# A two-layer decoder trunk on one core: sums of feed-forward weights moved from GpSimd to VectorE, and 13 instead of 15 blocks by the seven-product scheme

## The chip, the cores and the metric

The kernel runs on one core of a Trainium2 chip. The metric is device microseconds of one execution of the whole program, as a median over runs. The engines of the core are named as the profile names them: PE (TensorE, matrix products; PEld is its loading of weights), DVE (VectorE), ACT (ScalarE), POOL (GpSimd), and SP, which here only issues transfers. All engines run their own instruction stream in order and wait for each other by semaphores.

## The reference, cut to what matters

The program computes two decoder layers on a sequence of 512 tokens of width 1024, in float32. Each layer is an attention mixer followed by a feed-forward part, each with a norm in front and a residual added behind. Only the feed-forward part is touched by the change:

```
def rmsnorm(x, g):
    y = xf * lax.rsqrt(jnp.mean(xf * xf, axis=-1, keepdims=True) + NORM_EPS)
    return (y * g.astype(jnp.float32)).astype(x.dtype)

def swiglu(xn, w_gate, w_up, w_down):
    return (jax.nn.silu(xn @ w_gate) * (xn @ w_up)) @ w_down

    for layer in range(DEPTH):
        ...
        h = h + swiglu(rmsnorm(h, ffn_norm_g[layer]), ffn_w_gate[layer], ffn_w_up[layer], ffn_w_down[layer])
    return rmsnorm(h, final_norm_g)
```

The gate and up matrices are 1024 x 2816 each and the down matrix is 2816 x 1024, so a layer has 22 blocks of 128 hidden features.

## The kernel before

Activations lie transposed: 128 features on the partitions, 512 tokens along the free axis. Every float32 operand of a matrix product is held as two parts that the fast matmul type can take: a high part (ACT copies the value into that type) and a low part (DVE subtracts the high part from the value). A product of two such operands is three matmuls: high x high, high x low, low x high (`mm3`, L429; `product`, L919).

The function `ffn` (L851) computes a block of 128 hidden features in one of two ways.

*Direct* (`plain`, L864): for gate and for up, a slab of weights (128 x 1024) is loaded into `wraw`, split into `whl` (high by ACT, low by DVE, 1024 columns each), and multiplied with all eight chunks of the input `xo`: 24 matmuls of 512 columns for each of the two, 48 in all. DVE then scales the gate by the norm's factor `rbc`, ACT applies Silu, DVE multiplies with up, and the result is split into two parts again.

*By seven products* (`winograd`, L926): gate and up together form a 2 x 2 arrangement of blocks (gate and up against the two halves of the 1024 inputs), the input likewise (two halves of the features against two halves of the tokens). Strassen's scheme in Winograd's form needs seven products of half the size instead of eight: p1 to p7, each of 4 chunks x 3 matmuls of 256 columns, 84 matmuls in all. The price is sums. Those of the input are formed once per layer (`sums_of_x`, L884, into `tf`). Those of the weights are formed for each block: `a2` (tile `wu`) is the up slab, to whose first half a transfer adds its second half (L931, issued by POOL); then three POOL instructions of 512 columns each form `s23` (both halves) and `s4` (L939, L941, L944); the trace calls all of these `s`. The operands are then split: `w1` from the gate slab `a1` in `wraw`, `w3` from `s23`, `w2` from `a2` (one half of its low part by a second transfer that adds, L948), all into buffers `whl`, and `w4` from `s4` into `wf`. The products are evicted by one ACT copy and seven DVE additions of 256 columns (`add`, L959), after which come the scaling, Silu and the product of gate and up. The order on PE is p1, p6, p2, p7, p5, p4, p3; p6 and p7 use `w3`.

Before the change the blocks 0 and 1 of each layer are direct, 2 to 16 go by seven products, and 17 to 21 are direct. The results of the first six blocks are split at once into `hd`; the others wait as `hr` until the seven-product blocks are over and are split then (`later`, L986). The down projection follows, eight outputs with 22 x 3 matmuls each.

Buffers set how far ahead the operands can be made: two of `wraw`, four of `whl` (a seven-product block takes three, a direct one two), two of `wf`, three of `wu`, two of `s23`, two of `s4`.

No order of instructions is written by hand. `Sched` (L63) lists all operations with a cost and their dependences, simulates the engines, and writes each engine's stream in the order of that simulation. PE's operations have costs of their own there (`mm`, L356), DVE's are `vtt` (L243), POOL's `gtt` (L251), and the costs of DVE and POOL know nothing of each other.

Of the kernel before, what the change touches and what calls it, by code (L numbers as in the profile page):

```python
# [10 lines left out]
F32 = mybir.dt.float32  # L11
F32R = mybir.dt.float32r
# [3 lines left out]
OP = mybir.AluOpType  # L16
# [46 lines left out]
class Sched:  # L63
# [7 lines left out]
    def buf(self, tag):  # L71
        b = Buf(tag, len(self.queue[tag]))
        self.queue[tag].append(b)
        return b

    def op(self, alts, fn, r=(), w=(), dma=0, late=0.0):
        o = Op(len(self.ops), alts, fn, dma)
        o.late = late
        o.boost = self.boost
        self.ops.append(o)  # L80
        for toks, wr in ((r, False), (w, True)):
            for b, k in toks:
                if not b.ops or b.ops[-1] is not o:
                    b.ops.append(o)
                    o.bufs.append(b)
                lw, rd = b.tok.get(k, (None, []))
                if lw is not None and lw is not o:
                    o.pred.add(lw)
                if wr:
                    o.pred.update(x for x in rd if x is not o)  # L90
                    b.tok[k] = (o, [])
                else:
                    rd.append(o)
                    b.tok[k] = (lw, rd)
        return o
# [119 lines left out]
ENDED = {1: (), 2: (1,), 3: (1,), 4: (1, 3), 5: (1, 2, 3, 4), 6: (1, 2, 3, 4, 5), 7: (1, 2, 3, 4, 5),  # L215
         8: (1, 2, 3, 4, 5, 7)}
CLOSES = {1: (), 2: (1,), 3: (), 4: (3,), 5: (4, 2), 6: (5,), 7: (), 8: (7,)}
NP, NS, ND = 2, 15, 6
ORDER = ("Q0 Q1 A0 V1 Q2 A1 Q3 A2 V2 Q4 A3 Q5 A4 Q6 A5 Q7 V3 A6 A7",
         "Q0 V1 Q1 A0 Q2 A1 Q3 A2 V2 Q4 A3 Q5 A4 Q6 A5 Q7 V3 A6 A7")  # L220
LAT = 150.0
# [38 lines left out]
def trunk(ctx, tc, xT, pos, consts_in, gv, lamv, wv0, wqk0, wo0, wgu0, wd0, wv1, wqk1, wo1, wgu1, wd1, out):  # L260
    nc = tc.nc
    V, A, G, T = nc.vector, nc.scalar, nc.gpsimd, nc.tensor
    E = {"V": V, "A": A, "G": G, "T": T}

    AT, FK, FW, FH = (1, 5), (2, 6), (3, 7), (4, 8)
# [3 lines left out]
    def tag(name, shape, dt, n, scope=0):  # L269
        tags[name] = (scope, n)  # L270
        shapes[name] = (shape, dt)

    R5 = [128, 512]
# [17 lines left out]
    for L in range(2):  # L291
        sc = AT[L]
        for n, shp, dt, c in (("v", [128, 4, 2, 256], F32R, 2), ("sh", R5, F32, 2), ("a", R5, F32, 2),
                              ("kk", [128, 2, 512], F32R, 4), ("qs", R5, F32R, 4), ("lg", R5, F32, 4),
                              ("pt", [128, 2, 1664], F32R, 2), ("of", R5, F32, 1),
                              ("ot", [128, 2, 512], F32R, 8), ("col", [128, 4], F32, 8)):
            tag(f"{n}{L}", shp, dt, c, sc)
        if L == 1:
            tag("ss1", [128, 2, 512], F32R, 1, sc)
        else:  # L300
            tag("ma0", R5, F32, 1, sc)
        for sc, defs in ((FK, (("hd", [128, 2, 512], F32R, ND), ("hr", R5, F32, NP + NS - ND), ("rbc", R5, F32, 1),
                               ("cg", R5, F32, 2), ("cu", R5, F32, 2))),
                         (FW, (("tf", [128, 8256], F32R, 1), ("wf", [128, 2, 512], F32R, 2), ("wu", [128, 1024], F32, 3),
                               ("s23", [128, 1024], F32, 2), ("s4", R5, F32, 2))),
                         (FH, (("hh", [128, 2, 512], F32R, NF - ND),))):
            for n, shp, dt, c in defs:
                tag(f"{n}{L}", shp, dt, c, sc[L])

    S_ = Sched(tags, None)  # L310
    op, buf = S_.op, S_.buf
# [22 lines left out]
    def tt(e_alts, out_, a, b, o, n, r, w):  # L334
        op([(e, vtt(n) if e == "V" else gtt(n)) for e in e_alts],
           lambda e: E[e].tensor_tensor(out_(), a(), b(), o), r, w)  # L336
# [514 lines left out]
    def ffn(L, wgu, wd, gi_next):  # L851


        rbc = None
        ht = {}
# [2 lines left out]

        def parts(f, src, r):

            t = ht[f] = buf(f"hd{L}" if f < ND else f"hh{L}")
            split(lambda: t.t[:, 0, :], lambda: t.t[:, 1, :], src, 512, r, (t, 0), (t, 1), "V")

        def plain(f):  # L864
# [61 lines left out]
        def winograd(f):  # L926
            a1, a2, s23, s4 = buf("wraw"), buf(f"wu{L}"), buf(f"s23{L}"), buf(f"s4{L}")
            A1, A2 = wgu[2 * f], wgu[2 * f + 1]
            k1, k2 = slice(0, 512), slice(512, 1024)
            dma(lambda: a2.t, lambda: A2, (), [(a2, 0), (a2, 1)], 2 ** 19)  # L930
            op([("G", 1100)], lambda e: G.dma_start(a2.t[:, k1], A2[:, k2], accum_op=OP.add), [(a2, 0)], [(a2, 0)],  # L931
               dma=2 ** 19, late=4500.0)
            dma(lambda: a1.t, lambda: A1, (), [(a1, 0), (a1, 1)], 2 ** 19)
            w1, w3, w2, w4 = buf("whl"), buf("whl"), buf("whl"), buf(f"wf{L}")
            halves = lambda t: [(t, 0), (t, 1)]
            both = lambda w, src, n, r: split(lambda: w.t[:, 0, :], lambda: w.t[:, 1, :], lambda: src.t, n, r,
                                              (w, (0, 0)), (w, (1, 0)), "V")
            both(w1, a1, 1024, halves(a1))
            tt("G", lambda: s23.t[:, k1], lambda: a2.t[:, k1], lambda: a1.t[:, k1], OP.subtract, 512,  # L939
               [(a2, 0), (a1, 0)], [(s23, 0)])  # L940
            tt("G", lambda: s23.t[:, k2], lambda: a2.t[:, k2], lambda: s23.t[:, k1], OP.subtract, 512,  # L941
               [(a2, 1), (s23, 0)], [(s23, 1)])
            both(w3, s23, 1024, halves(s23))
            tt("G", lambda: s4.t, lambda: s23.t[:, k1], lambda: a1.t[:, k2], OP.subtract, 512, [(s23, 0), (a1, 1)],  # L944
               [(s4, None)])
            copy("A", lambda: w2.t[:, 0, :], lambda: a2.t, 1024, halves(a2), [(w2, (0, 0))])
            copy("A", lambda: w2.t[:, 1, k2], lambda: a2.t[:, k2], 512, [(a2, 1)], [(w2, (1, 1))], scale=-1.0)
            op([("G", 1100)], lambda e: G.dma_start(w2.t[:, 1, k2], A2[:, k2], accum_op=OP.add), [(w2, (1, 1))],  # L948
               [(w2, (1, 1))], dma=2 ** 19, late=4500.0)
            tt("V", lambda: w2.t[:, 1, k1], lambda: a2.t[:, k1], lambda: w2.t[:, 0, k1].bitcast(F32), OP.subtract, 512,  # L950
               [(a2, 0), (w2, (0, 0))], [(w2, (1, 0))])
            both(w4, s4, 512, [(s4, None)])
            p1, p6, p2, p7, p5, p4, p3 = [buf("ps_" + n) for n in "gsgtgos"]
            g, u = buf(f"cg{L}"), buf(f"cu{L}")
            P = lambda p: [(p, None)]
            q = lambda t: (lambda: t.t[:, :256])
            g0, g1, u0, u1 = [lambda t=t, k=k: t.t[:, k] for t in (g, u) for k in (lo_, up_)]

            def add(dst, a, p, tok, rd, o):  # L959
                tt("V", dst, a, q(p), o, 256, P(p) + rd, [tok])  # L960
            product(p1, w1, 0, xb(0, 0))
            copy("A", u0, q(p1), 256, P(p1), [(u, 0)], psum=True)
            product(p6, w3, 0, xt(1))
            add(g1, u0, p6, (g, 1), [(u, 0)], OP.add)
            product(p2, w1, 512, xb(1, 0))
            add(g0, u0, p2, (g, 0), [(u, 0)], OP.add)
            product(p7, w3, 512, xt(2))
            add(u0, g1, p7, (u, 0), [(g, 1)], OP.add)
            product(p5, w2, 0, xt(0))
            add(u1, u0, p5, (u, 1), [(u, 0)], OP.subtract)  # L970
            add(g1, g1, p5, (g, 1), [], OP.subtract)
            product(p4, w2, 512, xt(3), 1)
            add(u0, u0, p4, (u, 0), [], OP.add)
            product(p3, w4, 0, xb(1, 1))
            add(g1, g1, p3, (g, 1), [], OP.subtract)
            tt("V", lambda: g.t, lambda: g.t, lambda: rbc.t, OP.mult, 512, [(rbc, None)], halves(g))
            func(lambda: g.t, lambda: g.t, AF.Silu, 512, SET, [(g, 0), (g, 1)])
            if f < ND:
                tt("V", lambda: u.t, lambda: u.t, lambda: g.t, OP.mult, 512, halves(g), halves(u))
                parts(f, lambda: u.t, halves(u))  # L980
                return
            t = buf(f"hr{L}")
            tt("V", lambda: t.t, lambda: u.t, lambda: g.t, OP.mult, 512, halves(g) + halves(u), [(t, None)])
            return lambda: parts(f, lambda: t.t, [(t, None)])

        later = []  # L986
        for f in range(NF):
            if f == NP + NS:
                for x in later:
                    x()  # L990
            if f < NP or f >= NP + NS:
                plain(f)
                if f == 0:
                    sums_of_x()
            else:
                x = winograd(f)
                if x is not None:
                    later.append(x)
# [12 lines left out]
        for n in range(NC):  # L1011
# [9 lines left out]
            t = buf(f"cu{L}")  # L1021
# [213 lines left out]
```

## Time and profile before

| what | us |
|---|---|
| median of three runs | 1225.76 (1225.22 to 1231.3) |
| the profiled execution, its own time | 1226.0 |
| span of that execution, first to last instruction | 1224.1 |
| PE busy in the span | 1185.5 (97%) |
| DVE busy | 868.9 (71%) |
| ACT busy | 685.7 (56%) |
| POOL busy | 344.6 (28%) |
| gate and up products of layer 0, first direct block to last seven-product block | 253.39 to 438.64 |
| the same in layer 1 | 853.78 to 1035.81 |

The shares of the whole span are averages over stages with different limits. The change lies in two stretches of it, the two in the last rows, and those have to be read by themselves: what PE does there one product after another (the timeline), what the other engines are busy with in the same stretch (the windows), how long one and the same instruction takes at different moments (the instructions of a line), and what an idle engine waited for (the waits).

### The profile page before, as it was taken

The numbers are of one execution on the slowest core, as the hardware profiler recorded it, in microseconds if no ns is written. First come the engines' busy times: TensorE is split into PE (matmuls) and PEld (weight loads), VectorE is DVE, ScalarE is ACT, GpSimd is POOL, SyncE is SP. The second block draws the span as 40 slices with busy tenths as digits, with TensorE's granted clock in tenths as the row PEclk, the third lists the DMA queues.
The fourth block names the chain that finished last, engine by engine and source line by source line (L and its number), as shares of the span: only waits on it lengthen the run. The fifth ranks groups of instructions, "written<-read, shape, count | busy, mean of one in ns | idle before, by whom it ended". The sixth has DMA issues, their size and how long they took to land.

```text
span 1224.1 us, 19042 instructions
## 1 busy us (share of the span) xinstructions
PE 1185.5 (97%) x7074; PEld 1046.9 (86%) x7074; DVE 868.9 (71%) x1675; ACT 685.7 (56%) x1207; POOL 344.6 (28%) x292
## 2 busy tenths in 40 slices
PE   9999999998999999999999899999999999999997
PEld 7889788888999988888898787888899999888887
DVE  7876896679999974333246888975999999533333
ACT  7777987664454453222357788986745445432221
POOL 1222332255565400000021425322646561000000
PEclk9999999999999999999999999999999999999998
DMA  8775764554666443333578557555456663333322
GB/s 255 183 157 130 171 146 109 133 145 105 156 155 149 111 116 96 95 97 99 128 184 193 127 136 161 134 135 140 122 145 154 147 155 105 103 95 95 97 76 70
DMA packets 55916, 162.43 MB, mean 133 GB/s; under 512 B 6800, under 2 KB 10000, under 8 KB 55824
## 3 DMA queue, kind: packets, MB, share of 16 engines
q1 hardware_dynamic: 38832, 116.08, 30.7%
q0 software_dynamic: 16704, 45.10, 22.0%
q8 instruction: 56, 0.92, 0.3%
q14 instruction: 36, 0.29, 0.1%
q10 hardware_dynamic: 288, 0.04, 0.0%
HBM read 150.71 MB, written 2.10 MB: 125 GB/s over the span
## 4 chain that ended last, share of the span: by engine, by line
PE 49%; issue 21%; DVE 21%; DMA 4%; ACT 3%; POOL 1%; SPq 0%; DVEq 0%; POOLq 0%; ACTq 0%
PE ps_g L358 35%; PE ps_s L358 6%; DVE whl L336 5%; PE ps_o L358 3%; PE ps_t L358 3%; DVE cg L336 3%; DMA kk<-kk 2%; DVE cu L336 2%; PE ps_t L361 2%; DVE hr L336 2%; DVE lg L723 1%; DVE wf L336 1%; DVE lg L339 1%; DMA h<-xT 1%; DVE kk L336 1%
## 5 line engine op out<-in xcount | busy, mean ns | idle before, releaser
L358 PE MATMUL ps_g<-xo,whl 128*128 128x512 f32 (+1 forms) x2112 | 439.1, 356 | 0.0
L358 PEld LDWEIGHTS ps_g<-xo,whl 128*128 128x128 f32 x2112 | 346.4, 189 | 49.2
L327 ACT ACTIVATE whl<-wraw 128x1024 fp32r<-128x1024 f32 (+1 forms) x218 | 222.9, 1039 | 257.8 <-PE ps_g L358 181.9
L336 DVE TENSOR_TENSOR whl<-wraw,whl 128x1024 fp32r<-128x1024 f32 (+1 forms) x106 | 145.5, 1373 | 87.8 <-ACT whl L327 87.5
L358 PE MATMUL ps_g<-hh,whl 128*128 128x512 f32 (+1 forms) x816 | 177.7, 377 | 0.0
L358 PEld LDWEIGHTS ps_g<-hh,whl 128*128 128x128 f32 x816 | 146.9, 188 | 28.0
L358 PE MATMUL ps_g<-whl,xo 128*128 128x256 f32 x672 | 93.1, 288 | 0.0
L358 PEld LDWEIGHTS ps_g<-whl,xo 128*128 128x128 f32 x672 | 87.4, 193 | 1.3
L353 ACT ACTIVATE cg<-cg 128x512 f32<-128x512 f32 x44 | 27.6, 628 | 99.2 <-DVE cg L336 99.2
L353 ACT ACTIVATE lg<-lg,col 128x128 f32<-128x128 f32 (+3 forms) x128 | 70.8, 554 | 10.2 <-DVE col L723 9.0
L358 PE MATMUL ps_g<-ot,whl 128*128 128x512 f32 x288 | 73.6, 396 | 0.0
L396 POOL DMA_DIRECT2D whl<-wv x14 | 12.3, 879 | 200.8 <-ACT whl L327 199.8
L358 PE MATMUL ps_g<-hd,whl 128*128 128x512 f32 (+1 forms) x306 | 68.6, 377 | 0.0
L358 PE MATMUL ps_s<-kk,qs 128*128 128x128 f32 (+3 forms) x256 | 62.7, 327 | 5.2 <-DMA kk<-kk 4.7
L358 PEld LDWEIGHTS ps_g<-hd,whl 128*128 128x128 f32 x306 | 55.3, 188 | 10.6
L336 DVE TENSOR_TENSOR cu<-ps_g,rbc 128x512 f32<-128x512 f32 (+1 forms) x17 | 11.2, 660 | 72.4 <-PE ps_g L358 72.4
L358 PEld LDWEIGHTS ps_g<-ot,whl 128*128 128x128 f32 x288 | 52.9, 188 | 10.0
L358 PE MATMUL ps_s<-tf,whl 128*128 128x256 f32 x360 | 51.4, 285 | 10.3 <-DVE whl L336 8.5
L396 POOL DMA_DIRECT2D whl<-wqk x30 | 26.3, 878 | 109.9 <-ACT whl L327 72.0
L358 PEld LDWEIGHTS ps_s<-tf,whl 128*128 128x128 f32 x360 | 45.5, 188 | 13.7 <-DVE whl L336 11.5
L336 POOL TENSOR_TENSOR hr<-h,hr 128x256 f32<-128x256 f32 x4 | 2.8, 733 | 190.9 <-ACT hr L327 190.9
L336 POOL TENSOR_TENSOR sh<-sh,sk 128x512 f32<-128x512 f32 x28 | 38.7, 1383 | 60.1 <-DVE sh L682 48.3
(180 smaller groups left out, 2213.5 us busy)
## 6 DMA issues: line engine op xcount, KB each, us to landing
wraw<-wgu SPq DMA_DIRECT2D x58, 512.0 KB, 3.7
wraw<-wd SPq DMA_DIRECT2D x32, 512.0 KB, 3.5
wraw<-wqk SPq DMA_DIRECT2D x30, 512.0 KB, 6.8
whl<-wqk POOLq DMA_DIRECT2D x30, 512.0 KB, 7.4
wu<-wgu SPq DMA_DIRECT2D x30, 512.0 KB, 4.4
kk<-kk SPq DMA_DIRECT2D x64, 128.0 KB, 5.2
wraw<-wo SPq DMA_DIRECT2D x16, 512.0 KB, 5.2
wu<-wgu POOLq DMA_DIRECT2D x30, 256.0 KB, 4.3
```

What stands on the lines that cost most here:

```text
L327: A.activation(out_(), in_(), AF.Copy, scale=sc)
L336: lambda e: E[e].tensor_tensor(out_(), a(), b(), o), r, w)
L339: op([("V", vtt(n, 1))], lambda e: V.scalar_tensor_tensor(out_(), a(), s(), b(), o0, o1), r, w)
L353: A.activation(out_(), in_(), f, scale=scale, **kw)
L358: lambda e: T.matmul(out_(), l(), r_(), start=start, stop=stop), r, w)
L361: op([("T", 108)], lambda e: T.transpose(out_(), in_(), ident()), r + [(cc, None)], w)
L396: op([("G", 1100)], lambda e: G.dma_start(w.t[:, 1, :], src, accum_op=OP.add), [(w, (1, 0))], [(w, (1, 0))], dma=2 * 1024 * 512)
L723: op([("V", vtt(w) + 10)], lambda e: V.tensor_tensor_reduce(lg.t[:, :w], p.t[:, :w], mask[0]()[:, 512 - w:], -0.125, 3.0e38, OP.add, OP.mi ...
```

## The change

It does two things. The three sums of weights of a seven-product block (`s23`, both halves, and `s4`) are formed by DVE instead of POOL. And the blocks 2 and 9 of each layer are computed directly, so that 13 blocks in place of 15 go by seven products: 3 to 8 and 10 to 16. Six blocks are still split at once into `hd` (now 0 to 4 and 9), and eleven `hr` remain.

```diff
@@ -215,7 +215,10 @@
-NP, NS, ND = 2, 15, 6
+NW = 17
+PLAIN = (0, 1, 2, 9)
+DIRECT = (0, 1, 2, 3, 4, 9)
+ND = len(DIRECT)
@@ -299,7 +302,7 @@
-        for sc, defs in ((FK, (("hd", [128, 2, 512], F32R, ND), ("hr", R5, F32, NP + NS - ND), ("rbc", R5, F32, 1),
+        for sc, defs in ((FK, (("hd", [128, 2, 512], F32R, ND), ("hr", R5, F32, NW - ND), ("rbc", R5, F32, 1),
@@ -858,7 +861,7 @@
-            t = ht[f] = buf(f"hd{L}" if f < ND else f"hh{L}")
+            t = ht[f] = buf(f"hd{L}" if f in DIRECT else f"hh{L}")
@@ -936,12 +939,12 @@
             both(w1, a1, 1024, halves(a1))
-            tt("G", lambda: s23.t[:, k1], lambda: a2.t[:, k1], lambda: a1.t[:, k1], OP.subtract, 512,
+            tt("V", lambda: s23.t[:, k1], lambda: a2.t[:, k1], lambda: a1.t[:, k1], OP.subtract, 512,
                [(a2, 0), (a1, 0)], [(s23, 0)])
-            tt("G", lambda: s23.t[:, k2], lambda: a2.t[:, k2], lambda: s23.t[:, k1], OP.subtract, 512,
+            tt("V", lambda: s23.t[:, k2], lambda: a2.t[:, k2], lambda: s23.t[:, k1], OP.subtract, 512,
                [(a2, 1), (s23, 0)], [(s23, 1)])
             both(w3, s23, 1024, halves(s23))
-            tt("G", lambda: s4.t, lambda: s23.t[:, k1], lambda: a1.t[:, k2], OP.subtract, 512, [(s23, 0), (a1, 1)],
+            tt("V", lambda: s4.t, lambda: s23.t[:, k1], lambda: a1.t[:, k2], OP.subtract, 512, [(s23, 0), (a1, 1)],
                [(s4, None)])
@@ -975,7 +978,7 @@
-            if f < ND:
+            if f in DIRECT:
@@ -985,10 +988,10 @@
-            if f == NP + NS:
+            if f == NW:
                 for x in later:
                     x()
-            if f < NP or f >= NP + NS:
+            if f in PLAIN or f >= NW:
                 plain(f)
```

Since the scheduler writes the streams anew, the order around these instructions moves too; outside the two stretches it is the same on every engine. Three places follow. In the rows `whl`, `wf`, `wu`, `wraw`, `cg`, `cu` and `hr` are the buffers named above, `s_0_2511` and `s_1_2512` are the two buffers of `s23`, `s_0_2513` and `s_1_2514` those of `s4`; `ps_...` are accumulators of the products. Lines behind 218 stand three lower in the changed file (L339 is L336 of before).

DVE, layer 0, one seven-product block in the middle of the stretch, before, from the scaling of the finished block's gate on:

```order
L336 TENSOR_TENSOR cg_0_2497<-cg_0_2497,rbc_0_2496 128x512
L336 TENSOR_TENSOR cg_1_2498<-cu_1_2500,ps_s_85 128x256
L336 TENSOR_TENSOR hr_8_2493<-cu_0_2499,cg_0_2497 128x512
L336 TENSOR_TENSOR cg_1_2498<-cu_1_2500,ps_g_83 128x256
L336 TENSOR_TENSOR whl_73<-s_0_2511,whl_73 128x1024
L336 TENSOR_TENSOR cu_1_2500<-cg_1_2498,ps_t_88 128x256
L336 TENSOR_TENSOR whl_74<-wu_0_2508,whl_74 128x512
L336 TENSOR_TENSOR cu_1_2500<-cu_1_2500,ps_g_84 128x256
L336 TENSOR_TENSOR cg_1_2498<-cg_1_2498,ps_g_84 128x256
L336 TENSOR_TENSOR cu_1_2500<-cu_1_2500,ps_o_89 128x256
L336 TENSOR_TENSOR whl_75<-wraw_71,whl_75 128x1024
L336 TENSOR_TENSOR cg_1_2498<-cg_1_2498,ps_s_86 128x256
```

and in the changed kernel, a block of the same kind:

```order
L339 TENSOR_TENSOR cg_1_2498<-cg_1_2498,rbc_0_2496 128x512
L339 TENSOR_TENSOR cg_0_2497<-cu_0_2499,ps_s_85 128x256
L339 TENSOR_TENSOR s_1_2512<-wu_2_2510,wraw_71 128x512
L339 TENSOR_TENSOR hr_8_2493<-cu_1_2500,cg_1_2498 128x512
L339 TENSOR_TENSOR cg_0_2497<-cu_0_2499,ps_g_82 128x256
L339 TENSOR_TENSOR s_1_2512<-wu_2_2510,s_1_2512 128x512
L339 TENSOR_TENSOR whl_73<-s_0_2511,whl_73 128x1024
L339 TENSOR_TENSOR cu_0_2499<-cg_0_2497,ps_t_88 128x256
L339 TENSOR_TENSOR whl_74<-wu_1_2509,whl_74 128x512
L339 TENSOR_TENSOR cu_0_2499<-cu_0_2499,ps_g_83 128x256
L339 TENSOR_TENSOR cg_0_2497<-cg_0_2497,ps_g_83 128x256
L339 TENSOR_TENSOR cu_0_2499<-cu_0_2499,ps_o_89 128x256
```

The rest of the order is alike: the low part of `w3` behind the addition of p2, that of `w2` behind that of p7. Two sums (`s`), for the block after the next, now stand between the additions; the third follows behind the last row shown, ahead of the low part of `w1`.

POOL, the same stretch of layer 0, before:

```order
L948 DMA whl_72<-wgu 128x512
L336 TENSOR_TENSOR s_0_2511<-wu_0_2508,wraw_70 128x512
L336 TENSOR_TENSOR s_0_2511<-wu_0_2508,s_0_2511 128x512
L931 DMA wu_1_2509<-wgu 128x512
L336 TENSOR_TENSOR s_0_2513<-s_0_2511,wraw_70 128x512
L948 DMA whl_75<-wgu 128x512
L336 TENSOR_TENSOR s_1_2512<-wu_1_2509,wraw_71 128x512
L931 DMA wu_2_2510<-wgu 128x512
L336 TENSOR_TENSOR s_1_2512<-wu_1_2509,s_1_2512 128x512
```

and in the changed kernel, from the end of the input's sums on:

```order
L339 TENSOR_TENSOR hr_7_2492<-hr_7_2492,hr_4_2489 128x512
L339 TENSOR_TENSOR hr_6_2491<-hr_6_2491,hr_7_2492 128x512
L951 DMA whl_74<-wgu 128x512
L934 DMA wu_0_2508<-wgu 128x512
L951 DMA whl_73<-wgu 128x512
L934 DMA wu_1_2509<-wgu 128x512
```

All sums of weights are gone from POOL's stream, and only the issues of the adding transfers are left there; of the sums of the input (`hr`) five of the eight of a layer stand on POOL, where there were two.

DVE, layer 0, around the new direct block 9, in the changed kernel only (there is no such block in before): the first three rows and the `hr` belong to the end of block 7, the others to block 8 and to the operands made during it.

```order
L339 TENSOR_TENSOR whl_74<-wraw_70,whl_74 128x1024
L339 TENSOR_TENSOR cg_1_2498<-cg_1_2498,ps_s_86 128x256
L339 TENSOR_TENSOR cg_1_2498<-cg_1_2498,rbc_0_2496 128x512
L339 TENSOR_TENSOR cg_0_2497<-cu_0_2499,ps_s_85 128x256
L339 TENSOR_TENSOR hr_10_2495<-cu_1_2500,cg_1_2498 128x512
L339 TENSOR_TENSOR cg_0_2497<-cu_0_2499,ps_g_82 128x256
L339 TENSOR_TENSOR s_0_2511<-wu_0_2508,wraw_70 128x512
L339 TENSOR_TENSOR whl_75<-wraw_71,whl_75 128x1024
L339 TENSOR_TENSOR cu_0_2499<-cg_0_2497,ps_t_88 128x256
L339 TENSOR_TENSOR whl_72<-wraw_70,whl_72 128x1024
```

`whl_74` and `whl_75` are the two slabs of block 9, loaded by way of `wraw_70` and `wraw_71`. The buffer `wraw_70` is taken again for the gate slab of block 10, and the first sum for that block stands three additions behind the split that freed it.

## Rows read from the trace of the kernel before

**Rows 1.** Timeline of PE, both stretches: start, length, work, idle before and releaser.

```profile
264.15 14.63 PE L358 MATMUL ps_g<-xo,whl 128*128 128x512 f32 x69
...
284.89 1.64 PE L358 MATMUL ps_g<-tf,whl 128*128 128x256 f32 x12 [1.48 <-DVE cu L336]
...
292.12 1.44 PE L358 MATMUL ps_s<-tf,whl 128*128 128x256 f32 x10 [1.08 <-DVE whl L336]
...
428.67 1.60 PE L358 MATMUL ps_g<-xo,whl 128*128 128x256 f32 x12
...
438.64 54.59 PE L358 MATMUL ps_g<-xo,whl 128*128 128x512 f32 x240
493.07 4.24 PE L358 MATMUL ps_g<-hd,whl 128*128 128x512 f32 x18
...
864.84 14.64 PE L358 MATMUL ps_g<-xo,whl 128*128 128x512 f32 x69
...
1035.81 24.44 PE L358 MATMUL ps_g<-xo,whl 128*128 128x512 f32 x107
```

**Rows 2.** Windows, layer 0's seven-product blocks: length, busy time by engine (instructions), granted clock, transfers.

```profile
277.10:312.77 35.67, 31.52 (x255) 30.28 (x253) 34.93 (x43) 17.91 (x27) 17.41 (x15) 1.00 0.52 126
312.77:418.10 105.33, 101.32 (x843) 100.08 (x842) 102.61 (x130) 48.57 (x71) 64.28 (x51) 1.00 0.62 146
418.10:438.64 20.54, 20.20 (x170) 20.00 (x169) 18.57 (x33) 11.21 (x15) 1.75 (x2) 1.00 0.44 107
```

**Rows 3.** Instructions of DVE's line 336, layer 0: count, shortest, median, longest in ns.

```profile
L336 DVE TENSOR_TENSOR whl<-wraw,whl x19: 1208/1224/4399, 255.1 to 435.8; 128x1024 fp32r<-128x1024 f32 x19
L336 DVE TENSOR_TENSOR wf<-s,wf x15: 673/679/3218, 283.5 to 423.5; 128x512 fp32r<-128x512 f32 x15
L336 DVE TENSOR_TENSOR cg<-cu,ps_s x15: 403/408/422, 289.6 to 431.8; 128x256 f32<-128x256 f32 x15
```

**Rows 4.** Timeline of DVE and POOL side by side, an early block of layer 0.

```profile
284.67 4.40 DVE L336 TENSOR_TENSOR whl<-wraw,whl 128x1024 fp32r<-128x1024 f32 x1
...
285.10 1.63 POOL L336 TENSOR_TENSOR s<-wu,s 128x512 f32<-128x512 f32 x1
286.35 1.62 POOL L336 TENSOR_TENSOR s<-s,wraw 128x512 f32<-128x512 f32 x1
...
293.64 1.29 POOL L336 TENSOR_TENSOR s<-wu,wraw 128x512 f32<-128x512 f32 x1 [4.51 <-DMA wraw<-wgu]
```

**Rows 5.** Timeline of DVE and POOL, a block near the end, POOL forming no sums.

```profile
420.47 0.68 DVE L336 TENSOR_TENSOR whl<-wu,whl 128x512 fp32r<-128x512 f32 x1
...
420.83 0.88 POOL L948 DMA_DIRECT2D whl<-wgu  x1 [4.03 <-DVE cu L336]
...
423.53 0.68 DVE L336 TENSOR_TENSOR wf<-s,wf 128x512 fp32r<-128x512 f32 x1
424.13 0.68 DVE L336 TENSOR_TENSOR cg<-cg,rbc 128x512 f32<-128x512 f32 x1
...
425.51 0.69 DVE L336 TENSOR_TENSOR hr<-cu,cg 128x512 f32<-128x512 f32 x1 [0.37 <-ACT cg L353]
...
431.12 0.69 DVE L336 TENSOR_TENSOR cg<-cg,rbc 128x512 f32<-128x512 f32 x1
```

**Rows 6.** Waits of PE in layer 0's stretch: us in total, times, longest.

```profile
PE ps_s L358 <- DVE whl L336: 5.6, 7, 1.1
PE ps_g L358 <- DVE cu L336: 1.5, 1, 1.5
PE ps_s L358 <- ACT whl L327: 1.1, 2, 0.6
PE ps_o L358 <- DMA whl<-wgu: 0.2, 1, 0.2
```

**Rows 7.** Timeline of DVE at the entry of layer 0's stretch.

```profile
257.42 2.78 DVE L336 TENSOR_TENSOR hr<-hr,hr 128x512 f32<-128x512 f32 x3 [0.45 <-ACT hr L327]
```

**Rows 8.** Transfers by source: issuing queue, count, KB, median us to landing.

```profile
wraw<-wgu SPq DMA_DIRECT2D x58, 512.0 KB, 3.7
```

## The prediction

> **What bounds the kernel now.** PE is busy for 97% of the span, so I first looked at where it is not at its own pace. I read the timeline of PE through the two feed-forward stretches, then the windows over the seven-product blocks of layer 0, then the lengths of single DVE instructions there, and last the waits.
>
> The last seven-product block of layer 0 runs without a gap, from 428.67 to 438.64: 9.97 us is what PE needs for its 84 matmuls [rows 1]. The five direct blocks behind it take 438.64 to 493.07, 54.43 us, so 10.89 us each, or 0.2268 us a matmul [rows 1]. A seven-product block is thus worth only 0.92 us of PE's time.
>
> The first product of the first seven-product block starts 57 direct matmuls (12.93 us) into the rows at 264.15 and 864.84, so at 277.08 and 877.77. The 15 blocks end at 438.64 and 1035.81 [rows 1]. They take 161.56 and 158.04 us, 319.60 together. Thirty blocks at PE's pace would be 299.1. So **20.5 us are lost** in these stretches, 0.68 us a block. The clock is not the cause: it was granted in full [rows 2].
>
> What PE waits for there is mostly DVE: 5.6 us for the low parts of `whl` in front of p6 and p7 (the `w3` made from `s23`), 1.5 us for an addition that had to free an accumulator, and 1.1 us for ACT's high part of `w3`; a transfer accounts for 0.2 [rows 6]. Two such gaps stand in the timeline, 1.48 and 1.08 us [rows 1].
>
> DVE is the second bound. Over ten middle blocks it is busy 102.61 of 105.33 us, 10.26 us a block, more than the 9.97 that PE wants; POOL is busy 64.28 in the same time. In the last two blocks, where POOL does almost nothing (1.75 us), a block takes 10.27, and DVE has 2 us to spare [rows 2].
>
> Why 10.26? The same instruction has very different lengths. A low part of 1024 columns takes 1.21 us at its shortest and 4.40 at its longest, one of 512 columns 0.67 and 3.22; an addition that reads one operand from an accumulator keeps to 0.40 to 0.42 [rows 3]. The 4.40 us one began at 284.67 and ended when POOL's two sums, begun at 285.10 and 286.35, were over; those took 1.63 and 1.62, where one by itself takes 1.29 [rows 4]. So POOL's sums and DVE's two-operand instructions hold each other up.
>
> The Trainium skill says this too, in "SBUF — State Buffer", section "Who interferes with whom": a DVE instruction with two SBUF inputs contends with a GpSimd instruction that reads SBUF, and the loser blocks fully. The trace agrees for the pair at 284.67.
>
> **The change part by part.**
>
> *The three sums leave POOL.* A block of DVE's work without them can be read where POOL forms none: from one scaling of the gate (424.13) to the next (431.12) there are 6.99 us, 0.37 of it idle, so 6.62; that late no `wf` is split, which costs another 0.60 (423.53 to 424.13) [rows 5]. That makes 7.22, against 10.26 in the middle blocks. A transfer issued by POOL costs DVE nothing visible: beside the one at 420.83 DVE's two-operand instruction of 512 columns still took 0.68 [rows 5].
>
> *DVE takes them.* Three instructions of 512 columns with two operands, at the same 0.60 from start to start: 1.80. A block is then 7.22 + 1.80 = 9.02 us of DVE's time, 0.95 below PE's 9.97. Bounds: 9.02 if nothing inflates any more, and 10.26 + 1.80 = 12.06 if nothing shrinks. I take 9.02, because the cause of the inflation is gone from POOL's stream and not only less. PE is then the bound, and a block takes 9.97.
>
> *DVE now waits in order.* A sum needs two transfers to have landed; on POOL that wait (4.5 us once) held up nothing else, on DVE it holds up the additions behind it [rows 4]. In the middle blocks a sum for the block after the next stands in the order, and its gate slab's buffer was freed by the split at the end of the block before the previous one, some 10 us earlier, against 3.7 us to landing [rows 8]. Around the new direct block 9 only p3, p1, p6 and p2 lie between freeing and use, 4 x 1.42 = 5.7 us, less the split of 1.2: 4.5 us against 3.7 and the issue. I put 0.2 us per layer there, at most 0.95 before DVE's slack is gone.
>
> *Block 9 direct* also gives DVE some 6 us of rest: its own work is two low parts of 1024 columns and three instructions of 512, 4.3 us of 10.89.
>
> *Blocks 2 and 9 on PE:* 2 x 0.92 more per layer, 3.7 us together, wholly on the path.
>
> *The entry.* With block 2 direct, the first seven-product block starts 10.89 later, near 287.97. Up to its first addition, due at 287.97 + 2 x 1.42 = 290.8, DVE has in its order 33 instructions of 512 columns (19.8), five low parts of 1024 (6.1) and about 1 us of small ones: 26.9 us from 257.42 on [rows 7], so 284.3. Five sums of the input now run on POOL beside this, three more than before; if each held DVE up for its whole 1.6 us, the end would be 292.3. Between 0 and 1.5 us per layer, then; I take 0.3, since most of DVE's instructions there can pass between POOL's.
>
> *Waits for `w2`'s added low part* stay, about 0.2 us a layer [rows 6]. ACT and the mixers do the same work in the same order as before.
>
> *Sum.* After, without loss: 2 x (13 x 9.97 + 2 x 10.89) = 302.8 us against 319.6, so 16.8 less. Left over: 2 x (0.2 + 0.3 + 0.2) = 1.4. The profiled execution of 1226.0 becomes 1226.0 - 16.8 + 1.4 = 1210.6; the median is 0.24 below that execution, so **1210.4**.
>
> **The rivals.**
>
> *The entry stays slow.* In the first three blocks of layer 0, 35.67 us went where 29.9 were needed, a loss of 5.8, with DVE busy 34.93 of 35.67 [rows 2]. Layer 1 starts alike. If the longer queue of DVE at the entry keeps that loss, 2 x 5.8 come back: 1209.2 + 11.6 = 1220.6. Against it: PE gives DVE 10.89 us more before the first need.
>
> *No relief.* The loss is in the chain from transfer to sum to split, whoever forms the sum, and stays at 0.68 a block: 26 x 0.68 = 17.8, so 1227.0. For it: p6 also waited for ACT's copy of `s23`. Against it: the last two blocks run nearly free with the same chain but POOL quiet.
>
> *DVE becomes the bound, slower than before.* DVE is 97% busy in the middle blocks and gets more to do. If its instructions stay as long as they are, a block is 12.06 us of DVE's time; 26 x (12.06 - 9.97) = 54.3, so 1263.5. It decides against the change once a block of DVE's work is above 9.97 + 16.8 / 26 = 10.62, that is, when less than 1.44 of the 10.26 goes away. Against it: the 7.22 of a block without POOL's sums.
>
> This is what a rule of the Trainium skill would have led one to fear. "Perfetto Trace Analysis", section "Optimizing Scalar/DVE Operations", says that a saturated DVE may hand work to Scalar or even GPSIMD, though between DVE and GPSIMD this might not help because they share a read port. By the first half of that sentence the time would be 1263; by the second half, with which the 4.40 us row agrees, it is the forecast.
>
> **How the numbers follow.** The forecast, all relief with 0 to 5 us left over (1209 to 1214), gets 0.76. The entry rival gets 0.11, spread from 1214 to 1221; no relief 0.06; slower by DVE 0.07, from 1232 on. The range begins at 1207.5, below the 1209.0 of no loss at all by 1.5, because small waits ahead of these stretches may shrink too, and reaches to 1218, which takes in half of the entry rival. A measurement of this kernel can tell about 0.5%, 6.1 us, from no change, so faster means below 1219.6: 0.76 + 0.06 = 0.82. Same: the rest of the entry rival and no relief, 0.11. Slower: 0.07.
>
> **What would show it.** In the changed profile no DVE instruction of line 339 in the middle blocks should be much above 1.25 us (1024 columns) or 0.7 (512). PE's seven-product blocks should start every 9.97 us, also in the first three. DVE should be busy about nine tenths there, with waits for PE's products where it had none. PE's waits for `whl` should vanish. The forecast is wrong if DVE waits for `wraw` or `wu` with additions queued behind, if the entry still shows gaps in front of p6, or if `whl` instructions stay long with POOL idle.

## The result, and the profile after

The changed kernel takes 1211.61 us (median of four runs, 1210.52 to 1214.12); the kernel before took 1227.74 in the same comparison. The ratio is 0.9866, with a 95% interval of 0.9832 to 0.9899: 1.3% faster. Two further comparisons beside other kernels gave 1210.4 (ratio 0.9845, 0.9817 to 0.9874) and 1211.04 (0.984, 0.9814 to 0.9866). The forecast was 1210.4, with a range of 1207.5 to 1218.

PE is still the busiest engine, DVE and POOL have become shorter. The page, us busy, share of the span and instructions by engine, answers to the table of before (DVE 868.9, POOL 344.6):

```profile
PE 1183.7 (98%) x6930; PEld 1041.4 (86%) x6930; DVE 818.6 (68%) x1711; ACT 685.6 (57%) x1191; POOL 212.1 (17%) x200
```

The timeline of PE in the two stretches (start, length, work) answers to [rows 1]. Blocks 0 to 2 of each layer end in the rows that begin at 269.19 and 860.24, block 9 lies in the row at 352.93, and the rows at 433.65 and 1024.70 are block 17:

```profile
269.19 25.50 PE L361 MATMUL ps_g<-xo,whl 128*128 128x512 f32 x117
294.53 1.58 PE L361 MATMUL ps_s<-tf,whl 128*128 128x256 f32 x12
...
352.93 12.50 PE L361 MATMUL ps_g<-xo,whl 128*128 128x512 f32 x60
365.27 1.58 PE L361 MATMUL ps_s<-tf,whl 128*128 128x256 f32 x12
...
433.65 11.52 PE L361 MATMUL ps_g<-xo,whl 128*128 128x512 f32 x50
```

```profile
860.24 25.51 PE L361 MATMUL ps_g<-xo,whl 128*128 128x512 f32 x117
...
1024.70 45.52 PE L361 MATMUL ps_g<-xo,whl 128*128 128x512 f32 x200
```

No row between these carries an idle time. In layer 0 the stretch from the first direct block to the last seven-product block now takes 258.43 to 433.65, 175.22 us, in place of 185.25; in layer 1 849.64 to 1024.70, 175.06 in place of 182.03. That is 17.0 us less. The profiled execution gained only 11.9 (1226.0 to 1214.1), because the mixer of layer 0, whose code is the same, took 5 us longer in it: the stretch begins at 258.43 instead of 253.39. Three of the five are one longer wait of PE for a transfer between buffers of the keys, 5.5 us in place of 2.5 (the waits of PE over the whole span, before and after: us in total, times, longest):

```profile
PE ps_s L358 <- DMA kk<-kk: 4.7, 4, 2.5
```

```profile
PE ps_s L361 <- DMA kk<-kk: 7.4, 4, 5.5
```

Among the profiled executions of this study, all with the same code up to that point, the first stretch began anywhere between 251.83 and 258.43. Such a spread hides differences of a few us in a single profile; the stretches themselves, measured on PE's timeline, repeat within about 0.5 us, and I compare kernels by them below.

The windows over the seven-product blocks of layer 0 answer to [rows 2]: length, then busy time of PE, PEld, DVE, ACT and POOL with instruction counts, granted clock, share of transfers and GB/s. The second row is block 9:

```profile
293.10:352.93 59.83, 59.83 (x505) 59.83 (x504) 50.44 (x87) 31.09 (x41) 9.61 (x11) 1.00 0.70 163
352.93:363.80 10.87, 10.87 (x50) 9.01 (x49) 10.15 (x17) 4.95 (x7) 0.88 (x1) 1.00 0.38 112
363.80:433.65 69.85, 69.85 (x590) 69.81 (x590) 57.69 (x100) 35.58 (x46) 8.67 (x10) 1.00 0.54 126
```

PE is busy in every one of the 59.83 us, DVE in 50.44 of them, 84% in place of 97%. And the instructions of DVE's line 339 in layer 0 answer to [rows 3] (count; shortest, median, longest in ns):

```profile
L339 DVE TENSOR_TENSOR whl<-wraw,whl x22: 1218/1226/1717, 254.1 to 430.7; 128x1024 fp32r<-128x1024 f32 x22
L339 DVE TENSOR_TENSOR s<-wu,wraw x13: 679/686/693, 274.2 to 406.2; 128x512 f32<-128x512 f32 x13
...
L339 DVE TENSOR_TENSOR wf<-s,wf x13: 679/685/692, 282.8 to 415.0; 128x512 fp32r<-128x512 f32 x13
...
L339 DVE TENSOR_TENSOR cg<-cu,ps_s x13: 420/422/423, 296.2 to 426.8; 128x256 f32<-128x256 f32 x13
```

What took up to 4.40 and 3.22 us before now takes at most 1.72 and 0.69. The three of layer 0 that are still long (1.72 to 1.79 us, two of them in groups not shown) stand at the entry, between 275.97 and 281.70, beside POOL's sums of the input.

### The profile page after: what moved, and what is told of

The parts are those of the page before. It is cut to its first block, busy times and chain, and to the rows that moved or that the text cites. A ratio compares the mean times of both kernels' runs of the same rounds, so it can differ in the third digit from the quotient of the medians.

```text
span 1212.3 us, 18588 instructions
## 1 busy us (share of the span) xinstructions
PE 1183.7 (98%) x6930; PEld 1041.4 (86%) x6930; DVE 818.6 (68%) x1711; ACT 685.6 (57%) x1191; POOL 212.1 (17%) x200
## 4 chain that ended last, share of the span: by engine, by line
PE 70%; issue 16%; DVE 8%; DMA 4%; ACT 1%; SPq 0%; POOL 0%; POOLq 0%; ACTq 0%; DVEq 0%
PE ps_g L361 48%; PE ps_s L361 10%; PE ps_o L361 5%; PE ps_t L361 5%; DMA kk<-kk 2%; PE ps_t L364 2%; DVE lg L726 1%; DVE lg L342 1%; DMA h<-xT 1%; DVE pt L339 1%; DVE lg L334 1%; DVE kk L339 1%; DVE a L339 1%; DVE sh L685 1%; DVE qs L339 1%
## 5 line engine op out<-in xcount | busy, mean ns | idle before, releaser
L361 PE MATMUL ps_g<-xo,whl 128*128 128x512 f32 (+1 forms) x2208 | 470.1, 362 | 0.3 <-DVE v L342 0.3
L361 PEld LDWEIGHTS ps_g<-xo,whl 128*128 128x128 f32 x2208 | 370.4, 189 | 57.4 <-DVE v L342 0.5
L330 ACT ACTIVATE whl<-wraw 128x1024 fp32r<-128x1024 f32 (+1 forms) x222 | 227.4, 1041 | 293.0 <-PE ps_g L361 190.8
L339 DVE TENSOR_TENSOR whl<-wraw,whl 128x1024 fp32r<-128x1024 f32 (+1 forms) x110 | 131.3, 1194 | 97.9 <-ACT whl L330 97.3
L361 PE MATMUL ps_g<-hh,whl 128*128 128x512 f32 (+1 forms) x816 | 180.5, 377 | 0.0
L361 PEld LDWEIGHTS ps_g<-hd,whl 128*128 128x128 f32 x306 | 55.4, 188 | 10.6
L339 DVE TENSOR_TENSOR cu<-ps_g,rbc 128x512 f32<-128x512 f32 (+1 forms) x17 | 11.2, 660 | 72.4 <-PE ps_g L361 72.4
L361 PEld LDWEIGHTS ps_s<-kk,qs 128*128 128x128 f32 x256 | 43.9, 193 | 17.5 <-DMA kk<-kk 6.9
L726 DVE CUSTOM_DVE_ANT_0 lg<-ps_s,cc 128x128 f32<-128x128 f32 (+3 forms) x96 | 45.5, 484 | 14.5 <-PE ps_s L361 11.7
L951 POOL DMA_DIRECT2D whl<-wgu x26 | 22.7, 872 | 157.9 <-ACT whl L330 132.1
L339 POOL TENSOR_TENSOR sh<-sh,sk 128x512 f32<-128x512 f32 x28 | 38.7, 1382 | 60.3 <-DVE sh L685 48.6
L330 ACT ACTIVATE whl<-s 128x1024 fp32r<-128x1024 f32 x26 | 27.6, 1062 | 36.5 <-PE ps_g L361 30.0
L364 PE MATMUL ps_t<-cc,lg 128*128 128x128 f32 x240 | 40.4, 277 | 7.1 <-DVE lg L342 4.5
```

What stands on the lines that cost most here:

```text
L330: A.activation(out_(), in_(), AF.Copy, scale=sc)
L361: lambda e: T.matmul(out_(), l(), r_(), start=start, stop=stop), r, w)
L364: op([("T", 108)], lambda e: T.transpose(out_(), in_(), ident()), r + [(cc, None)], w)
L726: op([("V", vtt(w) + 10)], lambda e: V.tensor_tensor_reduce(lg.t[:, :w], p.t[:, :w], mask[0]()[:, 512 - w:], -0.125, 3.0e38, OP.add, OP.mi ...
```

## The experiments

**Which half of the change.** Three kernels undo one part each.

*The sums alone*: the kernel before, with 15 seven-product blocks, and the three sums on DVE.

```diff
-            tt("G", lambda: s23.t[:, k1], lambda: a2.t[:, k1], lambda: a1.t[:, k1], OP.subtract, 512,
+            tt("V", lambda: s23.t[:, k1], lambda: a2.t[:, k1], lambda: a1.t[:, k1], OP.subtract, 512,
...
-            tt("G", lambda: s23.t[:, k2], lambda: a2.t[:, k2], lambda: s23.t[:, k1], OP.subtract, 512,
+            tt("V", lambda: s23.t[:, k2], lambda: a2.t[:, k2], lambda: s23.t[:, k1], OP.subtract, 512,
...
-            tt("G", lambda: s4.t, lambda: s23.t[:, k1], lambda: a1.t[:, k2], OP.subtract, 512, [(s23, 0), (a1, 1)],
+            tt("V", lambda: s4.t, lambda: s23.t[:, k1], lambda: a1.t[:, k2], OP.subtract, 512, [(s23, 0), (a1, 1)],
```

> Only the first half of the change: the three sums of weights on VectorE, still 15 blocks by seven products (2 to 16). My theory: in the middle blocks a block of VectorE's work (9.02 us) fits under PE's 9.97, so they run without loss even without block 9's rest, which gains 2 x 2 x 0.92 = 3.7 us against the whole change. But the first seven-product block starts near 277 in place of 288, while VectorE's work before its first addition (26.9 us from 257.4 on) ends near 284: PE waits some 4 to 6 us per layer at the entry. Sum: 1211.6 - 3.7 + 8 to 12 = 1216 to 1220. Rival, the direct blocks are not needed at all: no gaps, 1208. Rival, the relief comes from the direct blocks: as the kernel before, about 1226.

Measured: 1208.45 us (ratio to before 0.9832, 0.9803 to 0.986), and beside the changed kernel once more:

> The kernel with the sums alone once more, beside the changed kernel on the same chip. By PE's stretches it is shorter by 3.1 us (347.6 against 350.7): expected 1207 to 1209 against 1210 to 1212, a difference of 0.25% that only the stretches can show surely.

1207.93 (0.9811, 0.9782 to 0.984), against 1211.04 for the changed kernel of the same group:

> The changed kernel beside it: 1210 to 1212, its two stretches 175.1 us each again.

The two intervals overlap, but the stretches don't: 173.77 and 173.87 us with the sums alone (173.49 and 173.95 the second time), against 175.22 and 175.06. My own theory had failed here: it expected PE to wait 4 to 6 us per layer at the entry. It waits for nothing there; its one wait in the stretch, 0.3 us, comes ahead of the seven-product blocks and is for the norm's factor. The timeline of PE and of DVE at the entry of layer 0 in this kernel, and the window over its 15 blocks, show how:

```profile
263.83 14.63 PE L358 MATMUL ps_g<-xo,whl 128*128 128x512 f32 x69
278.30 1.58 PE L358 MATMUL ps_s<-tf,whl 128*128 128x256 f32 x12
...
285.39 1.60 PE L358 MATMUL ps_s<-xo,wf 128*128 128x256 f32 x12
```

```profile
274.32 1.21 DVE L336 TENSOR_TENSOR whl<-s,whl 128x1024 fp32r<-128x1024 f32 x1
...
281.41 0.41 DVE L336 TENSOR_TENSOR cg<-cu,ps_s 128x256 f32<-128x256 f32 x1
```

```profile
276.80:426.45 149.65, 149.65 (x1261) 149.61 (x1261) 137.51 (x242) 80.66 (x108) 22.92 (x27) 1.00 0.63 151
```

The low part of `w3` (274.32) is ready before p6 starts at 278.30. The addition that takes p6's result comes late, at 281.41, some 1.5 us after p6's end at 279.88, and would have come later still if the scheduler had not put sums of later blocks behind it. PE does not notice: p6 and p3 take the two accumulators of that kind in turn, so p3 at 285.39 has the other one, and p6's is wanted again only by the next block's p6, ten us after the first. The 15 blocks take 149.65 us, 9.98 each, with PE busy throughout, while DVE is busy 9.17 a block.

*The blocks alone*: blocks 2 and 9 direct, the sums still on POOL (the changed kernel with the three `tt("V", ...)` above as `tt("G", ...)` again).

> Only the second half of the change: blocks 2 and 9 direct, the three sums of weights still on GpSimd. My theory: the sums of GpSimd and VectorE's two-operand instructions go on holding each other up, a middle block of VectorE's work stays near 10.26 us; the entry loses less, since the first seven-product block starts later. Between 1227 (the old loss of 0.68 us a block stays everywhere) and 1215.4 (the entry's loss of 5.8 us per layer is gone, the rest stays); I expect 1221. Rival, the direct blocks are what helps: 1211 to 1213, with long VectorE instructions but no gaps of PE.

Measured: 1216.23 us (0.9895, 0.9868 to 0.9921), between the bounds and better than expected. The stretches take 178.61 and 178.06, 10.6 less than before together. The windows of layer 0 (entry with block 2, six seven-product blocks, block 9), then DVE and POOL side by side:

```profile
268.00:289.88 21.88, 21.88 (x98) 18.12 (x97) 21.52 (x20) 11.27 (x20) 15.97 (x10) 1.00 0.18 56
289.88:350.96 61.08, 60.19 (x506) 59.95 (x505) 53.13 (x75) 30.91 (x43) 28.73 (x25) 1.00 0.66 160
350.96:361.90 10.94, 10.94 (x51) 9.04 (x50) 8.95 (x12) 4.68 (x7) 10.78 (x7) 1.00 0.29 73
```

```profile
316.93 3.12 DVE L339 TENSOR_TENSOR whl<-s,whl 128x1024 fp32r<-128x1024 f32 x1
```

```profile
317.32 1.63 POOL L339 TENSOR_TENSOR s<-wu,wraw 128x512 f32<-128x512 f32 x1
319.03 2.17 POOL L339 TENSOR_TENSOR s<-wu,s 128x512 f32<-128x512 f32 x1
```

The two engines still hold each other up: the split at 316.93 takes 3.12 us beside two sums. But the direct blocks give POOL time as well. It forms sums (two of them of the input) in 15.97 of 21.88 us at the entry and in 10.78 of 10.94 in block 9, so that fewer of them fall into the seven-product blocks (POOL is busy 28.73 us in six blocks, 4.8 a block with its issues, where ten blocks had 64.28), and DVE is busy only 8.9 us a block. Most of what is left of the loss has another place, in the waits of PE in layer 0's stretch:

```profile
PE ps_o L361 <- DMA whl<-wgu: 2.5, 2, 1.6
```

p4 waits for the low part that a transfer adds to `w2`, and POOL issues that transfer behind its sums.

*Block 9 by seven products again*, block 2 still direct:

```diff
-PLAIN = (0, 1, 2, 9)
-DIRECT = (0, 1, 2, 3, 4, 9)
+PLAIN = (0, 1, 2)
+DIRECT = (0, 1, 2, 3, 4, 5)
```

> The changed kernel with block 9 again by seven products: 14 such blocks (3 to 16), block 2 still direct, sums on VectorE. My theory: VectorE has 0.95 us to spare in every middle block, block 9's rest is not needed, and the direct block costs 2 x 0.92: 1211.6 - 1.8 = 1209.8, PE without a gap. Rival, VectorE falls behind block by block and needs block 9 to catch up: gaps of PE before p6 in the later blocks, 1212 or more.

Measured: 1209.19 us (0.9831, 0.9801 to 0.9861), beside the changed kernel itself:

> The changed kernel itself once more, beside the others of this group on one chip, as the mark they are compared with. Expected: 1211.6 us as at first, within 1210 to 1215; in the two feed-forward stretches PE again without a gap, 175.1 us each from the first direct matmul to the last seven-product block.

1210.4. The stretches: 174.30 and 174.67, against 175.21 and 175.53. PE has no gap in them, so the expectation held; block 9 costs 0.9 us a layer and gives nothing back.

In the stretches, then: the blocks alone win 10.6 us, the sums alone 19.6, both together 17.0. Since the gains do not add up, the two halves are two cures of one trouble, and after the better one the other only costs: 0.7 to 0.9 us per direct block.

**What the trouble was.** Two kernels add work for POOL to the changed kernel, once with reads of SBUF and once without. DVE has the same work in both.

```diff
+        dz = buf("sq")
...
+            for _ in range(3):
+                tt("G", lambda: dz.t, lambda: s23.t[:, k1], lambda: s23.t[:, k2], OP.subtract, 512,
+                   [(s23, 0), (s23, 1)], [(dz, None)])
```

> The changed kernel with three more instructions on GpSimd in each seven-product block: two-operand subtractions of 512 columns that read the block's sums (s23) and write a scratch tile nobody reads; nothing of the computation is left out. VectorE's work, its sums among it, is as in the changed kernel. My theory (GpSimd's reading and VectorE's two-operand instructions hold each other up): a block of VectorE's work grows from 9.0 us by the same 3.0 us as in the kernel before, to 12, above PE's 9.97; 26 blocks lose 2 us each, of which the rest in blocks 2 and 9 gives some back: 1245 to 1262. Rival (what was lost before was the chain from transfer to sum to split on the slow engine, not contention): no change, 1210 to 1213.

```diff
+            for _ in range(7):
+                op([("G", 540)], lambda e: G.memset(dz.t, 0.0), [(s23, 0), (s23, 1)], [(dz, None)])
```

> As the run with reads, but the extra work on GpSimd is seven memsets of 512 columns per block (about 0.69 us each, 4.9 us together, as much as three sums): it writes the scratch tile and reads nothing. My theory: VectorE's two-operand instructions keep their 1.22 and 0.68 us, PE keeps its pace; only the transfers that GpSimd issues may come later behind the memsets: 1210 to 1215. Rival (any work on GpSimd slows VectorE): as the run with reads.

Measured: 1233.43 us with reads (ratio to before 1.0016, 0.9993 to 1.004; one of its ten executions took 6697.71 us and is not in the ratio) and 1212.57 with writes (0.9856, 0.9811 to 0.99). The windows over the first six seven-product blocks of layer 0, reads first, then one and the same DVE instruction and POOL's added work in both kernels:

```profile
291.50:355.07 63.57, 61.49 (x507) 60.23 (x506) 61.59 (x88) 29.95 (x43) 32.32 (x26) 1.00 0.63 149
```

```profile
L339 DVE TENSOR_TENSOR whl<-wu,whl x13: 677/1450/1781, 293.5 to 433.1; 128x512 fp32r<-128x512 f32 x13
```

```profile
L339 POOL TENSOR_TENSOR sq<-s x39: 1286/1628/2747, 275.7 to 426.0; 128x512 f32<-128x512 f32 x39
```

```profile
291.30:351.18 59.88, 59.88 (x506) 59.84 (x506) 50.78 (x88) 31.11 (x41) 28.39 (x47) 1.00 0.70 165
```

```profile
L339 DVE TENSOR_TENSOR whl<-wu,whl x13: 681/683/691, 289.6 to 418.9; 128x512 fp32r<-128x512 f32 x13
```

```profile
L951 POOL MEMSET sq<- x91: 522/527/889, 275.4 to 412.4; 128x512 f32 x91
```

With reads the split of `wu` has a median of 1.45 us, with writes 0.68, and DVE's busy time over the six blocks is 61.59 of 63.57 us against 50.78 of 59.88, where the changed kernel had 50.44 of 59.83. POOL's busy time is not far apart, 32.32 and 28.39 us. So what stretches DVE's two-operand instructions is POOL's two-operand subtractions, which read, and not that POOL is busy or writes; a POOL instruction that reads one operand was not tried. That a chain from transfer to sum to split on a slow engine cost the time is ruled out for this part, since the sums stand on DVE here. Two things were not as I had said: a memset took 0.53 us, not 0.69, so that seven are 3.7 us and not as much as three reads (4.9); and the reads cost 22 us where I expected 34 at least. The stretches are 186.60 and 186.18 us long with reads, 175.48 and 175.82 with writes. One reason for the smaller cost is that DVE's work grew to 10.27 us a block over these six blocks, by 1.9 and not by 3.0.

Nor is all of the cost DVE's stretching. In the two stretches PE's waits for DVE's `cu` and `whl` come to 10.3 us, and 4.8 more are waits for the part that a transfer adds to `w2`, which POOL issues behind its added subtractions. And the longest wait also cost clock. It stands in block 10 and is for the multiplication on DVE that empties block 9's accumulator. The timeline of PE there and the window behind the wait:

```profile
375.90 2.90 PE L361 MATMUL ps_g<-tf,whl 128*128 128x256 f32 x12 [4.06 <-DVE cu L339]
```

```profile
376.00:378.00 2.00, 2.00 (x10) 2.00 (x11) 2.00 (x2) 2.00 (x4) 1.92 (x2) 0.50 0.88 131
```

PE had stood idle for 4.06 us; then its granted clock was 0.50, the lower of its two levels (1.2 of 2.4 GHz), and 12 matmuls took 2.90 us in place of 1.58. Layer 1 has the same, after 4.29 us.

**How much room DVE has.** Four kernels add two-operand subtractions of 512 columns on DVE, with `tt("V", ...)` in place of `tt("G", ...)` in the first of the two diffs above: one, three and four per block in the changed kernel, and four in the kernel with the sums alone.

> The changed kernel with one more two-operand subtraction of 512 columns on VectorE in each seven-product block, into a scratch tile nobody reads; nothing is left out. If a block of VectorE's work is 9.02 us and PE needs 9.97, 9.62 still fits: no change, 1210 to 1212, PE without gaps. Rival (VectorE, in order, has no real slack because it waits for products): 26 x 0.6 = 15.6 us more, 1226.

> The same with three more subtractions per block: 9.02 + 3 x 0.60 = 10.82 us of VectorE's work, 0.85 above PE's 9.97. My theory: VectorE is now the bound, 26 x 0.85 = 22 us, of which blocks 2 and 9 give back up to 6 us per layer: 1221 to 1233. Rival (the bound of PE holds whatever VectorE does in this range): 1211.

Measured: 1211.29 (0.9856, 0.9816 to 0.9896) and 1211.95 (0.9855, 0.9818 to 0.9892). The second was a miss: I expected 10 to 22 us. The windows of the kernel with three, over nearly all of the six blocks ahead of block 9, and about block 9:

```profile
293.10:351.70 58.60, 58.60 (x496) 58.60 (x496) 56.62 (x100) 30.25 (x41) 9.60 (x11) 1.00 0.69 162
351.70:363.00 11.30, 11.30 (x55) 9.48 (x54) 11.03 (x19) 4.95 (x7) 0.88 (x1) 1.00 0.43 121
```

DVE is busy 56.62 of 58.60 us, 9.6 a block and not 10.8. Since nothing waits for the results of the added subtractions, the scheduler had put some of them elsewhere: of layer 0's 39, 12 start in the first of these windows, five in the second (DVE is busy 11.03 of its 11.30 us) and four behind the last block. Four per block, in both kernels:

> The changed kernel with four more subtractions of 512 columns on VectorE per seven-product block (scratch tile, nothing left out). By the starts in the trace of the changed kernel a block of VectorE's work is 8.8 us, so this makes 8.8 + 4 x 0.60 = 11.2, 1.24 above PE's 9.97. Three more had cost nothing, since operands are made about a block ahead (some 8 us of lead) and block 9 gives some 6.6 us back. Six blocks before block 9 fall behind by 7.4, seven behind it by 8.7: I expect at most 2 us of gaps per layer, 1210 to 1216. Rival (VectorE is simply the bound, no lead): 26 x 1.24 = 32 us more, 1243.

> The same four on the kernel with the sums alone on VectorE and 15 seven-product blocks in a row. Falling behind is now 15 x 1.24 = 18.6 us per layer with no block to recover in, against about 8 us of lead: I expect 10 us of gaps per layer, 1208 + 20 = 1228 (1220 to 1236). This tells what the direct block 9 is worth: nothing at VectorE's present load, and a recovery when it is over PE's. Rival (the lead covers this too, or block 9 never matters): as after_plus_4 less 3, about 1209 to 1212.

Measured: 1211.72 (0.9845, 0.9812 to 0.9879) and 1234.21 (1.0037, 1.0015 to 1.0059). In the changed kernel PE waits among the seven-product blocks once, 0.3 us, per layer. Its window over the six blocks ahead of block 9:

```profile
287.03:346.86 59.83, 59.83 (x505) 59.82 (x504) 58.38 (x103) 29.95 (x40) 9.59 (x11) 1.00 0.68 165
```

DVE is busy 9.7 us a block there, still below PE's 9.97 and not 11.2: of the 24 subtractions that belong to these blocks only 15 start in them, since the scheduler put others ahead of the blocks, into block 9 and behind the last block. In the other kernel PE waits after the fifth block and then in every one; the timeline of PE (two of ten such rows), that of ACT, and the window behind:

```profile
421.19 1.45 PE L358 MATMUL ps_g<-xo,whl 128*128 128x256 f32 x10 [1.08 <-ACT cu L327]
...
432.43 1.45 PE L358 MATMUL ps_g<-xo,whl 128*128 128x256 f32 x10 [1.08 <-ACT cu L327]
```

```profile
420.75 0.38 ACT L327 ACTIVATE cu<-ps_g 128x256 f32<-128x256 f32 x1 [2.37 <-DVE hr L336]
```

```profile
350.00:440.00 90.00, 81.42 (x675) 79.80 (x674) 90.00 (x160) 41.73 (x58) 12.16 (x14) 1.00 0.51 123
```

PE's row names ACT, whose copy of p1 into `cu` it waits for; ACT's row names DVE, for which that copy had itself waited 2.37 us. So it is DVE, by way of ACT. From one such row to the next there are 11.24 us, as much as the 11.2 that DVE's instructions add up to, and DVE is busy in all of the 90 us. So DVE sets the pace when its work is above PE's 9.97 us a block, but only after the lead in operands is used up, five blocks long here. The direct blocks of the changed kernel, at the entry and in the middle, took in part of the added work; which of the two does more was not tried. That a lead alone carries DVE's 11.2 us through the changed kernel is not shown, since its seven-product blocks never held that much.

## Why the prediction was right, point by point

*PE's pace and the loss.* Right. Without DVE's stretching PE runs all 26 seven-product blocks at 9.97 us, the first three too, and the direct ones at 10.9. The waits of [rows 6] add up to 8.4 of the 12.0 us that layer 0's 15 blocks lost; the other 3.6 stand in no wait, PE being counted as busy in them, and they went away with the rest.

*The sums leave POOL, DVE takes them.* Right in kind and size. The prediction took 9.02 us of DVE's work a block; DVE is busy 8.4 a block over the six blocks ahead of block 9, and 9.17 in the kernel with 15 such blocks in a row. That DVE takes over the pace above PE's 9.97 was shown by the four added subtractions in the kernel with the sums alone. The cause, POOL's reads beside DVE's two-operand instructions, was shown by reads against writes. It is what the Trainium skill states in "SBUF — State Buffer", section "Who interferes with whom", where a GpSimd instruction that only writes is also said not to contend: the trace agrees, 1.45 us beside reads and 0.68 beside memsets.

*Two readings of the rows were loose.* The split of 4.40 us did not end when POOL's two sums were over: the second ended at 286.35 + 1.62 = 287.97 and the split at 289.07, 1.10 us later [rows 4]. That is nearly the 1.21 us that it takes by itself, so the reading of the cause stands: the split seems to have done little while the sums ran. And the 1.5 us wait of PE was not for an addition of a seven-product block but for the multiplication that empties the accumulator of the direct block 1. DVE's row, just ahead of the long split:

```profile
284.07 0.68 DVE L336 TENSOR_TENSOR cu<-ps_g,cg 128x512 f32<-128x512 f32 x1
```

*DVE waits in order around block 9.* Right, and free. The place was predicted, with at most 0.95 us of DVE's time. The timeline of DVE at the end of block 8 shows the wait for the gate slab of block 10, in layer 0 only:

```profile
348.75 0.69 DVE L339 TENSOR_TENSOR s<-wu,wraw 128x512 f32<-128x512 f32 x1 [0.87 <-DMA wraw<-wgu]
```

PE lost nothing by it; I had put 0.2 us a layer.

*The entry.* Wrong, though without harm to the sum (0.3 us a layer expected, none found). The step that failed is "its first addition, due at 287.97 + 2 x 1.42": an addition is not due for PE when its product ends, but when its accumulator is wanted again, by the next block's p6 some ten us later (no row of [rows 6] was a wait for such an addition). In the changed kernel DVE even had time to spare: it waited 1.39 us for the last direct product and 0.23 us for p6 before that addition, which began at 296.22. With that the whole argument for block 2 falls, and the rival of a slow entry with it: the kernel with the sums alone starts its seven-product blocks without block 2's help and has no gap, though its first addition comes 1.5 us after p6's end.

*Waits for `w2`'s added part.* None is left (0.2 us a layer expected). With the sums in POOL's queue (the blocks alone) they are 2.5 us in layer 0.

*The sum.* The stretches became 17.0 us shorter where 16.8 - 1.4 = 15.4 had been forecast; the 1.4 were the three waits above, all zero. The medians of one comparison, 1227.74 and 1211.61, are 16.1 us apart. That the median itself is within 1.2 us of 1210.4 is partly luck: the stretches gained 1.6 us more than forecast, and the kernel before gave 1225.76 in one comparison and 1227.74 in the next.

*Blocks 2 and 9.* The price of 3.7 us was somewhat high: 2.6 us in the stretches by the kernel with the sums alone (2.8 to 3.1 beside the changed kernel's other two profiles). What the prediction did not see is that nothing is bought with it: it counted block 9's rest and the later entry as helps, and neither was needed at DVE's present work. They are room for more of it: block 9 took in some of the added subtractions.

*A version better than both* is the one with the sums alone, 1207.9 to 1208.5 us. Its gain over the changed kernel is 0.2%, sure by the stretches and not by the medians.

## What to carry to other kernels

When one engine's instructions of one shape have very different lengths, look at what its neighbour does at that moment before believing the busy share: here POOL's three sums saved DVE 1.8 us of work a block and stretched the rest of it by 3.0 (DVE busy 10.26 a block before, [rows 2], for work of 7.22 at the short lengths). Taking the work back onto an engine that is 97% busy can be right if that share is inflated. And of a change with two cures for one wait, try each alone: the second may only cost.

## What the runs showed of the hardware

- A two-operand DVE instruction of 512 columns took 0.68 us beside POOL's memsets of 0.53 us, and a median of 1.45 in the kernel with POOL's two-operand subtractions, whose own median was 1.63 where the shortest took 1.29.
- Adding transfers issued by POOL did not lengthen DVE's instructions (0.68 us beside one, [rows 5]), but they stand in one queue with POOL's other work: PE waited up to 1.6 us for one behind POOL's sums.
- After PE had stood idle for 4.06 us its granted clock was 0.50, and 12 matmuls of 256 columns took 2.90 us in place of 1.58.
- The same code ahead of the first stretch took between 251.83 and 258.43 us in fourteen profiled executions; where the difference arises beyond the one wait for `kk` shown above was not looked into.
